# A seven-product matrix step starts two feature tiles earlier in the second layer, its right factors handed over one by one

## Chip, core and metric

The kernel runs on one core of one Trainium2 chip. The metric is device time in microseconds (us) from launch to end, and the median of several runs is compared. The engines are named as in the profile: PE is TensorE (PEld its weight loads), DVE is VectorE, ACT is ScalarE, POOL is GpSimd, and SP issues most of the loads.

## What is computed

Two layers of a backbone over 512 latent tokens and 256 context tokens, 1024 features wide; the second layer keeps the latent tokens only. Each layer has a mixer part (not touched here) and this feed-forward part, where `h` is the normed and modulated stream:

```python
D_FF = 2816
def conv_ffn(h, w_up, conv_w, w_down):
    up = h @ w_up
    a, b = up[..., :D_FF], up[..., D_FF:]
    return (jax.nn.silu(dwconv3(a, conv_w)) * b) @ w_down
```

All of it is float32, and the kernel keeps that precision: every operand of a large product is split into a high and a low part, `hi` and `lo`, and a product is three passes, hi·hi, lo·hi and hi·lo.

## The kernel before

Features lie on the partitions, tokens run along the free axis. The 2816 hidden features are 22 tiles of 128 (`f` = 0 to 21). Each tile needs its `a` rows and its `b` rows of `w_up`: two weight units of 128 x 1024 numbers, one for `a` and one for `b`.

**A plain tile.** One unit is 8 blocks of the contraction x 3 passes = 24 matmuls of 512 columns. ACT casts the unit's high part (`wh`, line 276), DVE or POOL subtracts to get the low part (`wl`, lines 286 and 288). Behind the product `a`, `gate`/`up_a` run the convolution (two DVE instructions, line 302) and the SiLU on ACT; behind `b` DVE multiplies (line 286), and `hidden` splits the result into `hi` (ACT) and `lo` (DVE).

**A quad.** Two neighbouring tiles together are a 2 x 2 block product, which `quad` (line 629) does with seven half-size products in place of eight: 7 products x 4 blocks `q` of the contraction x 3 passes = 84 matmuls of 256 columns for `a`, 84 for `b`. The left factors are sums of the weights, made by `split_quad` (line 614): four DVE additions `wr<-wr` of 128 x 512, and the high and low parts of four units (`.0` to `.2` of 1024 columns, `.3` of 512, named `s4h` and `s4l`). The right factors are made by `right_factors` (line 584) once per layer from the modulated stream: for each of the four `q`, `t13` and `t24` are sums of quarters (four DVE instructions of 256 columns), `t24` is split into `th` and `tl` (factors t2 and t4), half of `t13` into `t3`. Three factors are parts of `h2` as they are (b11, b21, b22). The last, t1, is split **in place** over the second half of `h2`'s first tile (`hhi`, `hlo`), so it must wait until no plain tile reads that half any more. `quad` uses them in the order b11, t2, t1, t3, b21, b22, t4.

Which tiles are plain is `PLAIN` (line 1856): the first layer starts quads at `f` = 4, the second at 6. The second layer's four first units (`f` = 0, 1) run as one batch in two halves while the stream is still being made; then come the plain tiles one after the other, then the quads. The down projection of a finished chunk comes one chunk later.

**What sets the order.** A scheduler (`Sched`, line 81) runs at build time. Strands of work (Python generators) yield instructions; it keeps a model of when each engine is free, and lets the strand with the lowest priority number go first among those that are ready. Each engine's order in the program is the result and is fixed on the chip. `K.when` holds a strand until its condition is true at build time. `PRF` (line 1845) is the priority of `right_factors` for each layer; splitting of weights has 2, the convolutions and multiplications 1. A low part that may go to DVE or POOL goes where the model ends it earlier.

There are 5 buffers each for `wh` and `wl` and 4 for the raw units, so a unit can be cast only when the unit five before it is done.

Of the kernel before, what the change touches and what calls it, by code (L numbers as in the profile page):

```python
# [54 lines left out]
def quads(l, f):  # L55

    return l in QUADS and f >= PLAIN[l]

# [386 lines left out]
def build(tc, a, out):  # L445
    nc = tc.nc
    es = ExitStack()
    with es:
# [9 lines left out]
        K = Sched(nc)  # L458
# [319 lines left out]
        def passes(w, h):  # L778
            return ((w[0], h[0]), (w[0], h[1]), (w[1], h[0]))
# [544 lines left out]
        def layer(l):  # L1324
# [3 lines left out]
            T = SEQ if last else TOK  # L1328
# [218 lines left out]
            quad_b, quad_t = {}, {}  # L1547
# [34 lines left out]
            H = T // 2  # L1582

            def right_factors():

                for q in range(4):
                    (hi1, lo1), (hi2, lo2) = h2[2 * q], h2[2 * q + 1]
                    yield from K.when(lambda: all((2 * q + i, g[0]) in h2.done for i in range(2) for g in halves))
                    if BACT:
                        yield from K.when(lambda: all(len(wholes.get(2 * q + i, ())) == 2 for i in range(2)))  # L1590
                        b1, b2 = wholes[2 * q][0], wholes[2 * q + 1][0]
                    else:
                        b1 = yield from S.get("b1")
                        yield from K.tt(b1[:, 0:T], hi1[:, 0:T], lo1[:, 0:T], ALU.add, ("pool",))
                        b2 = yield from S.get("b2")
                        yield from K.tt(b2[:, 0:T], hi2[:, 0:T], lo2[:, 0:T], ALU.add, ("pool",))
                    t13 = yield from S.get("t13")
                    yield from K.tt(t13[:, 0:H], b1[:, 0:H], b1[:, H:T], ALU.subtract)
                    yield from K.tt(t13[:, H:T], b1[:, H:T], b2[:, H:T], ALU.subtract)
                    S.put(b1)  # L1600
                    t24 = yield from S.get("t24")
                    yield from K.stt(t24[:, 0:H], t13[:, 0:H], -1.0, b2[:, H:T], ALU.mult, ALU.subtract)
                    yield from K.tt(t24[:, H:T], b2[:, 0:H], t24[:, 0:H], ALU.add)
                    S.put(b2)
                    th = yield from S.get("th", F32R)
                    tl = yield from S.get("tl", F32R)
                    yield from K.split(th[:, 0:T], tl[:, 0:T], t24[:, 0:T])
                    S.put(t24)
                    t3 = yield from S.get("t3", F32R)
                    yield from K.split(t3[:, 0:H], t3[:, H:T], t13[:, H:T])  # L1610
                    quad_t[q] = (t13, th, tl, t3)
                yield from K.when(lambda: state.get("plain") == l)
                for q in range(4):
                    t13, th, tl, t3 = quad_t[q]
                    (hi1, lo1), (hi2, lo2) = h2[2 * q], h2[2 * q + 1]
                    yield from K.split(hi1[:, H:T], lo1[:, H:T], t13[:, 0:H])
                    S.put(t13)
                    quad_b[q] = dict(b11=(hi1[:, 0:H], lo1[:, 0:H]), t1=(hi1[:, H:T], lo1[:, H:T]),
                                     b21=(hi2[:, 0:H], lo2[:, 0:H]), b22=(hi2[:, H:T], lo2[:, H:T]),
                                     t2=(th[:, 0:H], tl[:, 0:H]), t4=(th[:, H:T], tl[:, H:T]), t3=(t3[:, 0:H], t3[:, H:T]))  # L1620
                quad_t["free"] = [t for q in range(4) for t in quad_t[q][1:]]

            def product(bank, w, off, b, first):
                for q in range(4):
                    yield from K.when(lambda: q in quad_b)
                    yield from K.mms([(bank[:, 0:H], wp[:, off + 128 * q:off + 128 * q + 128], bp, first and q == 0 and i == 0,
                                       q == 3 and i == 2) for i, (wp, bp) in enumerate(passes(w, quad_b[q][b]))], not first)

            def quad(key, post):

                at, bk = set(), {}

                def prod(bank, w, off, b, name, first):
                    if first:
                        bk[bank] = yield from P.get(bank, 1)
                    yield from product(bk[bank], w, off, b, first)
                    at.add(name)
                K.spawn(post(bk, at), 1)
                g0 = yield from unit(key + ".0")
                yield from prod("x", g0, 0, "b11", "p1", True)  # L1640
                g1 = yield from unit(key + ".1")
                yield from prod("y", g1, 512, "t2", "p6", True)
                yield from prod("z", g1, 0, "t1", "p5", True)
                unit_done(g1)
                g2 = yield from unit(key + ".2")
                yield from prod("w", g2, 0, "t3", "p7", True)
                yield from K.when(lambda: "x read" in at)
                yield from prod("x", g0, 512, "b21", "p2", False)
                unit_done(g0)
                g3 = yield from unit(key + ".3")  # L1650
                yield from K.when(lambda: "z read" in at)
                yield from prod("z", g3, 0, "b22", "p3", False)
                S.put(*g3)
                yield from K.when(lambda: "w read" in at)
                yield from prod("w", g2, 512, "t4", "p4", False)
                unit_done(g2)
# [74 lines left out]
            if l in QUADS:  # L1731
                K.spawn(right_factors(), PRF[l])

# [108 lines left out]
STRICT = True  # L1842
PAL = 3.5
BACT = True
PRF = (1.5, 2.5)
MB0 = 3
AVALL = True
SWC = 0.09
# [4 lines left out]
EARLY = True  # L1853
RLQ = ('pool',)
ADAG = 2
PLAIN = (4, 6)
PADA = 2
ENDCTX = False
LA = 4
# [137 lines left out]
```

## Time and profile before

| | us |
|---|---|
| median of 3 runs | 1461.02 |
| lowest and highest run | 1459.94 and 1463.81 |
| the profiled execution, its own time | 1462.63 |
| its span in the profile | 1460.9 |

The span runs from the first to the last instruction in the profile; the execution's own time has 1.7 us more around it. In the timeline rows the first number is the start in us from the span's start, the second the time until the instruction has ended. Instructions of one engine overlap at their ends, so what one costs a busy engine is the distance from its start to the next one's start.

### The profile page before, as it was taken

The page shows a single profiled execution, that of the slowest core. Times are in us where ns is not written, and L with a number is a line of the kernel's source. Part 1 is how long each engine was busy: PE and PEld are TensorE (multiplying, and loading weights), DVE is VectorE, ACT ScalarE, POOL GpSimd, SP SyncE. Part 2 cuts the span into 40 slices and gives each one's busy share as a digit, 9 for nine tenths or more (in the row PEclk, how much of TensorE's full clock was granted, in tenths as well). Part 3 has the DMA queues.
Part 4 walks back from the last instruction along what each step waited for, and adds up shares of the span by engine and source line. Part 5 has one row for each costly group of instructions (what it writes and reads, how often), then busy time and mean ns, then how long its engine had stood idle before and what let it go on. Part 6 is the DMA issues. An engine that isn't in the chain of part 4 may idle for free.

```text
span 1460.9 us, 23874 instructions
## 1 busy us (share of the span) xinstructions
PE 1414.9 (97%) x9196; PEld 1265.8 (87%) x9196; DVE 1119.2 (77%) x1899; ACT 754.5 (52%) x1216; POOL 369.7 (25%) x456
## 2 busy tenths in 40 slices
PE   6999999999999999999999999998999999999997
PEld 4877888788898999999999988876789899999987
DVE  4748578767997788897777878798886767778885
ACT  5446456425543455454545444647646456656652
POOL 0231453111212122211222114476220012221130
PEclk9999999999999999999999999999999999999998
DMA  9495152224046588656886834434242267787771
GB/s 373 152 319 180 50 145 70 91 84 162 30 144 152 140 214 204 178 154 200 225 214 189 285 126 138 144 116 154 78 144 75 90 140 152 177 182 171 171 203 59
DMA packets 75538, 229.12 MB, mean 157 GB/s; under 512 B 10624, under 2 KB 12800, under 8 KB 75296
## 3 DMA queue, kind: packets, MB, share of 16 engines
q0 software_dynamic: 36256, 103.44, 29.9%
q1 hardware_dynamic: 36576, 121.67, 24.6%
q10 hardware_dynamic: 2592, 2.49, 0.5%
q8 instruction: 72, 1.18, 0.3%
q14 instruction: 42, 0.34, 0.1%
HBM read 164.64 MB, written 51.38 MB: 148 GB/s over the span
## 4 chain that ended last, share of the span: by engine, by line
PE 83%; DVE 7%; DMA 4%; issue 3%; POOL 1%; ACT 1%; SPq 0%; DVEq 0%; POOLq 0%; ACTq 0%
PE banks L234 82%; DMA adaw<-in_w_ada 2%; PE banks L247 2%; DVE mx L328 1%; DVE wl L286 1%; DMA stk<-rhi 1%; DMA x<-in_xT 0%; DVE shuf L286 0%; DMA wr<-in_w_dn 0%; DVE ropey L286 0%; POOL p L317 0%; DVE p L302 0%; POOL avr L1056 0%; DVE mlo L286 0%; DVE by L302 0%
## 5 line engine op out<-in xcount | busy, mean ns | idle before, releaser
L234 PE MATMUL banks<-hhi,wh 128*128 128x512 f32 (+2 forms) x968 | 301.3, 335 | 1.3 <-DVE oT L286 1.1
L276 ACT CAST wh<-wr 128x1024 fp32r<-128x1024 f32 x220 | 229.2, 1046 | 139.9 <-PE banks L234 85.2
L234 PE MATMUL banks<-hlo,wh 128*128 128x512 f32 (+2 forms) x968 | 298.5, 333 | 0.4 <-DVE hlo L302 0.3
L234 PE MATMUL banks<-hhi,wl 128*128 128x512 f32 (+2 forms) x968 | 297.7, 332 | 0.0
L286 DVE TENSOR_TENSOR wl<-wr,wh 128x1024 fp32r<-128x1024 f32 x189 | 230.5, 1222 | 74.2 <-ACT wh L276 61.6
L216 POOL DMA_DIRECT2D xacc<-ev x128 | 111.3, 870 | 364.0 <-ACT ev L315 359.6
L234 PEld LDWEIGHTS banks<-hhi,wh 128*128 128x128 f32 x968 | 173.1, 189 | 19.1 <-issue 3.4
L234 PEld LDWEIGHTS banks<-hlo,wh 128*128 128x128 f32 x968 | 173.2, 189 | 15.7 <-DVE hlo L302 2.6
L234 PEld LDWEIGHTS banks<-hhi,wl 128*128 128x128 f32 x968 | 173.0, 189 | 14.1 <-DVE wl L286 0.3
L234 PE MATMUL banks<-lo,wh 128*128 128x512 f32 (+1 forms) x560 | 171.0, 347 | 3.8 <-DVE lo L286 3.8
L234 PE MATMUL banks<-hi,wh 128*128 128x512 f32 (+1 forms) x560 | 171.3, 348 | 0.0
L234 PE MATMUL banks<-hi,wl 128*128 128x512 f32 (+1 forms) x560 | 170.2, 346 | 0.0
L315 ACT ACTIVATE ev<-banks,ada 128x512 f32<-128x512 f32 x192 | 111.6, 616 | 82.1 <-PE banks L234 58.8
L234 PEld LDWEIGHTS banks<-lo,wh 128*128 128x128 f32 x560 | 96.2, 190 | 18.1 <-DVE lo L286 5.1
L234 PEld LDWEIGHTS banks<-hi,wh 128*128 128x128 f32 x560 | 96.4, 189 | 13.8 <-ACT hi L276 0.2
L234 PEld LDWEIGHTS banks<-hi,wl 128*128 128x128 f32 x560 | 96.1, 189 | 14.1
L288 POOL TENSOR_TENSOR wl<-wr,wh 128x1024 fp32r<-128x1024 f32 (+1 forms) x31 | 77.4, 2504 | 117.0 <-ACT wh L276 89.6
L286 DVE TENSOR_TENSOR wr<-wr 128x512 f32<-128x512 f32 x136 | 91.1, 694 | 3.7 <-DMA wr<-in_w_up 3.0
L203 POOL DMA_DIRECT2D adaw<-in_w_adaT x56 | 34.2, 623 | 220.2 <-DVE adaw L302 158.7
L234 PE MATMUL banks<-th,wl 128*128 128x384 f32 (+1 forms) x272 | 84.4, 310 | 0.0
L234 PE MATMUL banks<-tl,wh 128*128 128x384 f32 (+1 forms) x272 | 84.4, 310 | 0.0
L234 PE MATMUL banks<-th,wh 128*128 128x384 f32 (+1 forms) x272 | 84.3, 310 | 0.0
(240 smaller groups left out, 3064.5 us busy)
## 6 DMA issues: line engine op xcount, KB each, us to landing
wr<-in_w_up SPq DMA_DIRECT2D x88, 512.0 KB, 3.8
adaw<-in_w_adaT POOLq DMA_DIRECT2D x56, 512.0 KB, 6.5
xacc<-ev POOLq DMA_DIRECT2D x64, 384.0 KB, 9.8
wr<-in_w_dn SPq DMA_DIRECT2D x44, 512.0 KB, 6.3
xacc<-ev POOLq DMA_DIRECT2D x64, 256.0 KB, 7.8
adaw<-in_w_ada SPq DMA_DIRECT2D x40, 384.0 KB, 7.6
wr<-in_w_zt SPq DMA_DIRECT2D x24, 512.0 KB, 5.0
wr<-in_w_o SPq DMA_DIRECT2D x16, 512.0 KB, 3.5
```

The source lines that it names most:

```text
L203: yield from self.op([(q, cost[q], lambda q=q: eng[q].dma_start(out, in_)) for q in queues], outs, ins)
L216: yield from self.op([("pool", 0.9, lambda: self.nc.gpsimd.dma_start(out, in_, accum_op=ALU.add))], [], [in_])
L234: self.nc.tensor.matmul(o, l, r, start=a, stop=b, skip_group_check=more)
L247: self.nc.tensor.transpose(o, i, ident)
L276: opts.append(("act", 0.19 + n / 1200, lambda: self.nc.scalar.copy(out, in_)))
L286: opts.append(("dve", 0.15 + n / 960, lambda: self.nc.vector.tensor_tensor(out, a, b, op=op)))
L288: opts.append(("pool", 0.1 + n * 2.25e-3, lambda: self.nc.gpsimd.tensor_tensor(out, a, b, op=op)))
L315: emit = dict(act=lambda: self.nc.scalar.activation(out, a, AF.Copy, scale=s), dve=lambda: self.nc.vector.tensor_scalar(out, a, s, None, o ...
L328: lambda: self.nc.vector.tensor_reduce(out, in_, axis=AX.X, op=op), [out], [in_])
```

## The change

Three edits:

- `quad_b[q]` is filled as soon as the factors of `q` are made, all but t1; t1 is added after its split in place. `product` waits for the one factor it needs, not for all.
- `PRF` of the second layer falls from 2.5 to 1, ahead of the splitting of weights.
- `PLAIN` of the second layer falls from 6 to 4: tiles 4 and 5 become the first quad, right behind plain tile 3.

```diff
                     quad_t[q] = (t13, th, tl, t3)
+                    quad_b[q] = dict(b11=(hi1[:, 0:H], lo1[:, 0:H]), b21=(hi2[:, 0:H], lo2[:, 0:H]),
+                                     b22=(hi2[:, H:T], lo2[:, H:T]), t2=(th[:, 0:H], tl[:, 0:H]),
+                                     t4=(th[:, H:T], tl[:, H:T]), t3=(t3[:, 0:H], t3[:, H:T]))
                 yield from K.when(lambda: state.get("plain") == l)
...
                     S.put(t13)
-                    quad_b[q] = dict(b11=(hi1[:, 0:H], lo1[:, 0:H]), t1=(hi1[:, H:T], lo1[:, H:T]),
-                                     b21=(hi2[:, 0:H], lo2[:, 0:H]), b22=(hi2[:, H:T], lo2[:, H:T]),
-                                     t2=(th[:, 0:H], tl[:, 0:H]), t4=(th[:, H:T], tl[:, H:T]), t3=(t3[:, 0:H], t3[:, H:T]))
+                    quad_b[q]["t1"] = (hi1[:, H:T], lo1[:, H:T])
...
-                    yield from K.when(lambda: q in quad_b)
+                    yield from K.when(lambda: b in quad_b.get(q, ()))
...
-PRF = (1.5, 2.5)
+PRF = (1.5, 1)
...
-PLAIN = (4, 6)
+PLAIN = (4, 4)
```

In the built program nothing moves in the first layer: all engines have the same instructions in the same order up to the second layer's feed-forward part, and again from its second quad on. Between them three places matter.

On VectorE, in the second layer's feed-forward part, behind the batch of tiles 0 and 1 (`fy<-banks,vec` is the convolution of an `a` tile, `fy<-banks,fy` the multiplication with a `b` tile, `wl` a low part of a weight unit, `t13`/`t24` the sums for the right factors). Before:

```order
L302 SCALAR_TENSOR_TENSOR fy_10993<-banks_77,vec_81,fy_10993 128x511 x2
L286 TENSOR_TENSOR wl_11007<-wr_10575,wh_10996 128x1024
L302 SCALAR_TENSOR_TENSOR fy_10995<-banks_77,vec_81,fy_10995 128x511 x2
L286 TENSOR_TENSOR fy_10993<-banks_77,fy_10993 128x512
L286 TENSOR_TENSOR wl_11034<-wr_10692,wh_11006 128x1024
L286 TENSOR_TENSOR lo_11040<-fy_10993,hi_11039 128x512
L286 TENSOR_TENSOR fy_10995<-banks_77,fy_10995 128x512
L286 TENSOR_TENSOR wl_11053<-wr_10728,wh_11033 128x1024
```

and with the change, from the same convolution on:

```order
L302 SCALAR_TENSOR_TENSOR fy_11012<-banks_77,vec_81,fy_11012 128x511 x2
L286 TENSOR_TENSOR tl_11011<-t24_11007,th_11010 128x512
L302 SCALAR_TENSOR_TENSOR fy_11014<-banks_77,vec_81,fy_11014 128x511 x2
L286 TENSOR_TENSOR t13_11041<-x4_9945 128x256
L286 TENSOR_TENSOR t13_11041<-x4_9945,x5_9950 128x256
L302 SCALAR_TENSOR_TENSOR t24_11051<-t13_11041,x5_9950 128x256
L286 TENSOR_TENSOR t24_11051<-x5_9950,t24_11051 128x256
L286 TENSOR_TENSOR fy_11012<-banks_77,fy_11012 128x512
L286 TENSOR_TENSOR fy_11014<-banks_77,fy_11014 128x512
L286 TENSOR_TENSOR tl_11059<-t24_11051,th_11058 128x512
L286 TENSOR_TENSOR t3_11080<-t13_11041,t3_11080 128x256
```

The three low parts that VectorE made here for the units `b` of tile 2 (`wr_10575`), `a` of tile 3 (`wr_10692`) and `b` of tile 3 (`wr_10728`) are gone from this stretch; the factor work of `q` = 1 and 2 stands in their place. Eleven rows further down, behind the factor work of `q` = 3, the third of them follows, and from there to the low halves of the factor split in place stand:

```order
L302 SCALAR_TENSOR_TENSOR fy<-banks,vec,fy 128x511 x2
L286 TENSOR_TENSOR fy<-banks,fy 128x512
L286 TENSOR_TENSOR wl<-wr,wh 128x1024
L286 TENSOR_TENSOR lo<-fy,hi 128x512
L286 TENSOR_TENSOR wl<-wr,wh 128x1024
L286 TENSOR_TENSOR wr<-wr 128x512 x4
L286 TENSOR_TENSOR wl<-wr,wh 128x1024
L302 SCALAR_TENSOR_TENSOR fy<-banks,vec,fy 128x511 x2
L286 TENSOR_TENSOR wl<-wr,wh 128x1024
L286 TENSOR_TENSOR s4l<-wr,s4h 128x512
L286 TENSOR_TENSOR wl<-wr,wh 128x1024
L286 TENSOR_TENSOR hlo<-t_10991,hhi 128x256
```

The first `wl` of these rows is the low part for `b` of tile 3 (`wr_10728`), the second unit `.0` of the first quad, `wr<-wr x4` the additions for that quad, and the next `wl`, `wl` and `s4l` its units `.1` to `.3`; the last `wl` is unit `.0` of the quad's `b` half. `hlo` is the first low half of t1. Before it stood behind the matmuls of a down projection, now it stands behind plain tile 3 with no other work of PE than the first two products of the quad between them.

On GpSimd, in the same place, between the last write of the stream and the first addition of the down projection:

```order
 L203 DMA xacc_80<-x_9964 128x256
 L203 DMA xacc_80<-x_9969 128x256
-L288 TENSOR_TENSOR wl<-wr,wh 128x1024
+L288 TENSOR_TENSOR t_11030<-t_11004,t_11030 128x256
+L288 TENSOR_TENSOR wl<-wr,wh 128x1024 x2
+L288 TENSOR_TENSOR hlo<-t_11087,hhi 128x256
 L216 DMA xacc_80<-ev 128x512 x64
```

GpSimd made one low part here (for `a` of tile 4); now it makes the low part of `t3` for `q` = 1, then the low parts for `b` of tile 2 and `a` of tile 3, then the last low half of t1.

## Rows read from the trace of the kernel before

**Rows 1.** The page: the span, busy time by engine, the chain that ended last
```profile
span 1460.9 us, 23874 instructions
PE 1414.9 (97%) x9196; PEld 1265.8 (87%) x9196; DVE 1119.2 (77%) x1899; ACT 754.5 (52%) x1216; POOL 369.7 (25%) x456
PE 83%; DVE 7%; DMA 4%; issue 3%; POOL 1%; ACT 1%; SPq 0%; DVEq 0%; POOLq 0%; ACTq 0%
```
**Rows 2.** Timeline of PE: first plain tile, first down projection, first quad, next down projection
```profile
1117.46 0.40 PE L234 MATMUL banks<-hhi,wh 128*128 128x512 f32 x1
...
1161.85 0.40 PE L234 MATMUL banks<-hi,wh 128*128 128x512 f32 x1
...
1184.11 0.28 PE L234 MATMUL banks<-hhi,wh 128*128 128x256 f32 x1
...
1187.27 0.28 PE L234 MATMUL banks<-hhi,wh 128*128 128x256 f32 x1
1187.63 0.39 PE L234 MATMUL banks<-hlo,wh 128*128 128x256 f32 x1
...
1204.21 0.40 PE L234 MATMUL banks<-hi,wh 128*128 128x512 f32 x1
```
**Rows 3.** Timeline of DVE behind the batch, and where it made right factors
```profile
1117.32 1.53 DVE L302 SCALAR_TENSOR_TENSOR fy<-banks,vec,fy 128x511 f32<-128x511 f32 x2 [5.06 <-ACT fy L266]
1118.77 1.22 DVE L286 TENSOR_TENSOR wl<-wr,wh 128x1024 fp32r<-128x1024 f32 x1
1119.90 1.53 DVE L302 SCALAR_TENSOR_TENSOR fy<-banks,vec,fy 128x511 f32<-128x511 f32 x2
...
1132.33 0.69 DVE L286 TENSOR_TENSOR tl<-t,th 128x512 fp32r<-128x512 f32 x1
1132.93 0.42 DVE L286 TENSOR_TENSOR t<-t,t 128x256 fp32r<-128x256 f32 x1
1133.26 0.42 DVE L286 TENSOR_TENSOR t<-x 128x256 f32<-128x256 f32 x1
```
**Rows 4.** Timeline of ACT in the same stretch
```profile
1116.59 0.69 ACT L266 ACTIVATE fy<-banks,vec 128x512 f32<-128x512 f32 x1 [5.92 <-PE banks L234]
1117.18 1.04 ACT L276 CAST wh<-wr 128x1024 fp32r<-128x1024 f32 x1
...
1120.22 0.63 ACT L266 ACTIVATE fy<-fy 128x512 f32<-128x512 f32 x1
...
1126.82 0.61 ACT L276 CAST th<-t 128x512 fp32r<-128x512 f32 x1
1130.10 0.40 ACT L276 CAST t<-t 128x256 fp32r<-128x256 f32 x1
```
**Rows 5.** POOL: one form (count, busy us, mean ns, idle); POOL and DVE in time
```profile
L288 POOL TENSOR_TENSOR ss<-ss,sq 128x256 f32<-128x256 f32 x4 | 2.9, 729 | 60.4 <-ACT sq L266 60.3
...
1126.01 1.53 DVE L302 SCALAR_TENSOR_TENSOR fy<-banks,vec,fy 128x511 f32<-128x511 f32 x2
1126.05 2.40 POOL L288 TENSOR_TENSOR wl<-wr,wh 128x1024 fp32r<-128x1024 f32 x1 [34.84 <-ACT wh L276]
```
**Rows 6.** Timeline of DVE and POOL where both subtract from SBUF
```profile
891.02 3.41 POOL L288 TENSOR_TENSOR wl<-wr,wh 128x1024 fp32r<-128x1024 f32 x1
892.05 2.92 DVE L286 TENSOR_TENSOR ropey<-ropey,shuf 128x512 f32<-128x512 f32 x1
...
958.57 4.95 POOL L288 TENSOR_TENSOR wl<-wr,wh 128x1024 fp32r<-128x1024 f32 x2
961.18 2.88 DVE L286 TENSOR_TENSOR shuf<-shuf,sin 128x512 f32<-128x512 f32 x1
```
**Rows 7.** Stretches by engine (us, PE, PEld, DVE, ACT, POOL busy, PEclk, DMA share, GB/s)
```profile
1085.00:1092.00 7.00, 4.58 (x45) 4.21 (x43) 6.44 (x15) 5.54 (x11) 1.84 (x4) 0.93 0.46 164
1092.00:1098.00 6.00, 6.00 (x27) 5.74 (x28) 3.88 (x8) 2.14 (x6) 0.00 (x0) 0.51 0.56 182
```
**Rows 8.** Timeline of PE: the matmul in front of that stretch, with the wait
```profile
1091.56 0.44 PE L234 MATMUL banks<-ss,mats 128*32 128x64 f32 x8 [2.42 <-DVE ss L286]
```

## The prediction

> **What bounds the kernel now.** I read the page first: TensorE is busy for 97% of the span, and the chain that ended last is TensorE for 83% [rows 1]. So time is won where TensorE has less to do, and lost where it waits. Next I read TensorE's timeline around the change. From 1117.46 to 1161.85 us it runs the second layer's eight plain units (tiles 2 to 5) without a gap: 44.39 us, 5.549 us for a unit and 0.231 us for each of its 24 matmuls. The first quad takes from 1184.11 to 1204.21, 20.10 us for 168 matmuls [rows 2]. In it one matmul starts 0.36 us behind the one in front, where 0.118 is usual (1187.27 and 1187.63): it waited 0.25 us for the low half of the factor that is split in place. Without that wait a quad takes 19.85 us. Then I read VectorE and ScalarE, which make what TensorE needs: at 1117.32 VectorE comes out of 5.06 us of idleness, and then it works closely packed [rows 3]. A small fall in its pace is hidden; a delay of several us isn't.
>
> In the first layer the change moves nothing, so handing the factors over early is worth nothing there: the places of the instructions are the same. All of it is decided between 1110 and 1165 us.
>
> **What TensorE saves.** Removed: tiles 4 and 5, four units of 5.549 us, 22.20 us. Added: one quad, 19.85 us. Gain 2.35 us. The old quad's wait of 0.25 goes too, because its in-place split is long done by then: **2.60 us**. The down projections and the other eight quads stay, and the loads on SP's queue keep their order and sizes. That sum holds if TensorE is fed as before.
>
> **What VectorE needs, and when.** The costs as distance between starts [rows 3]: a convolution 1.45 us (two instructions), a low part `wl` 1.13 (1.22 until its result is there), a 512-column instruction 0.60, a 256-column one 0.33; the four that make `t13` and `t24` take 1.46, since two wait for each other. On ScalarE a convolution's first step or a SiLU takes some 0.6, a cast 0.94, 0.61 or 0.40 by size [rows 4].
>
> The idle time up to 1117.3 now takes the factors of q = 0 and the sums of q = 1; that costs nothing. Then, in the new order: convolution (to 1118.77), `tl` (1119.37), convolution (1120.82). Meanwhile ScalarE has made the first convolution step from 1116.59, a cast, `th`, the second convolution step and the high part of t3: 1116.59 + 0.59 + 0.94 + 0.53 + 0.59 + 0.40 = 1119.6. GpSimd takes its low part (as 256 columns, 0.73 us) and right behind it the low part for `b` of tile 2 (2.40 us): 1120.4 to 1122.8 [rows 5]. TensorE needs that at 1117.46 + 5.55 + 2 x 0.23 = 1123.5, so it is in time by 0.7.
>
> **But VectorE isn't free in that time.** At 1120.8 its next instruction is a subtraction of two SBUF tensors, and GpSimd is inside one. What then happens is in the trace: at 892.05 such a VectorE instruction took 2.92 us, and one at 961.18 2.88, for 512 columns that take 0.69 [rows 6, 3]. Both times it ended 0.6 us behind GpSimd's instruction, so it had stood until that was through; and GpSimd's took 3.41 instead of 2.40 when it came second [rows 6, 5]. A convolution, which has one operand in PSUM, isn't slowed and doesn't slow GpSimd: 1.53 and 2.40 us side by side at 1126 [rows 5]. So VectorE stands from 1120.8 to 1122.8 (2.0 us), and again when GpSimd takes the low part for `a` of tile 3, which ScalarE has cast at about 1123.0: 2.4 us more. The four sums end at 1122.8 + 2.4 + 1.46 = 1126.7.
>
> The Trainium skill says in GPSIMD Engine Reference (section Specifications) that GpSimd shares its SBUF interfaces with VectorE and that VectorE instructions with two SBUF inputs contend; it doesn't say that one stands for the whole of the other. If the two only shared, each at half pace, VectorE would by my estimate lose some 1.5 us here and not 4.4, TensorE would wait 1.8 us at the split in place, and the sum would be -0.8. Rows 6 show the whole instruction waited out, and the measurement decides.
>
> From there: two multiplications (1.2), `tl` and the wait for ScalarE's cast (0.6 + 0.5), t3 (0.33), the sums of q = 3 (1.55), two `lo` (1.2), `tl` (0.6), t3 (0.33), convolution (1.53 until its end), SiLU on ScalarE with both hand-overs (0.7), multiplication (0.6), and only then the low part for `b` of tile 3 (1.22): 1126.7 + 10.4 = **1137.1**. TensorE wants it at 1117.46 + 3 x 5.549 + 0.46 = 1134.57. Before it was made ahead of all factor work. **TensorE waits 2.5 us.**
>
> VectorE goes on without a pause: `lo` 0.6, `wl` 1.13, four additions 2.4, `wl` 1.13, convolution 1.45, `wl` 1.13, `s4l` 0.6, `wl` 1.13, together 9.6 us, then the first low half of t1: 1146.6 + 0.42 = 1147.0. Without any wait TensorE would want it in the third product, at 1139.66 + 24 x 0.118 + 0.1 = 1142.6. That is 4.4 us late, of which 2.5 are waited already. The last two of the four low halves come from both engines, and one of them waits for the other's 0.73 us. So behind the third product TensorE is late by 4.4 + 0.7 = **5.1 us**. After that it isn't late again: the quad's next need of VectorE lies three products, 4 us, further on, and the down projection behind it gives VectorE slack.
>
> **Sum without the clock:** 5.1 - 2.6 = 2.5 us slower.
>
> **The clock.** After a wait of 2.42 us at 1091.56 the granted clock of the stretch 1092 to 1098 was 0.51, so 1.2 GHz where it is 2.4 otherwise [rows 8, 7]. At half pace 6 us of it lose 3. A wait of 2.5 us for `b` of tile 3 can do the same, or nothing: the bounds are 0 and 3 us. Most of it is hidden: TensorE would come to the third product at 1142.6 + 2.5 + 3 = 1148.1 and find its factors ready at 1147 to 1148.5, so it is late by 5.5 and not by 5.1 + 3. I take 0.4 us more, and keep 0 and 3.
>
> **2.5 + 0.4 = 2.9 us slower:** from the profiled execution's 1462.63 us that is 1465.5, and from the median of the runs, which is 1.6 lower, 1461.02 + 2.9 = **1463.9 us**. About 0.3%, 4.4 us, is what can be told from no change here; this is under it.
>
> **The rivals.**
>
> *The gain comes.* GpSimd and VectorE don't meet, because one of them starts a little earlier or later or because the waits are shorter than in rows 6. Then the chain on VectorE is 4.2 us earlier: the low part for `b` of tile 3 is ready at 1132.9, in time by 1.7, the first low half of t1 at 1142.9, late by 0.3. The time is 1461.0 - 2.6 + 0.3 = 1458.7 us. For it: there is 5.06 us of idleness that the factors now fill [rows 3]. Against: GpSimd's start at 1120.4 hangs on ScalarE alone, whose rows up to there are known, and VectorE's next free instruction comes 0.4 us later. Chance 0.2. Even this doesn't reach 4.4 us.
>
> *Slower for good: the clock falls behind the second wait.* The price of the clock is hidden only if it falls at the first wait. Where TensorE keeps 2.4 GHz through the first wait and then stands another 2 to 2.6 us at the third product, a fall there has no wait to hide in: 5.1 + 3 - 2.6 = 5.5 us, 1466.5 us. It decides if two waits within 13 us are followed by a granted clock near 0.5 behind the second alone. For it: 2.42 us sufficed once [rows 8, 7]. Against: the first wait is as long as the second. Chance 0.18.
>
> *Nothing comes of it* because something other than TensorE sets the end, a load or the additions of the last down projection: 1461.0. Against it stands the share of TensorE in the chain [rows 1]. Chance 0.04.
>
> **How the numbers follow.** My forecast has 0.58, and its own range is 1462.0 to 1465.2 (the clock at 0, the waits half a us shorter, or both longer by 0.8). Most of it and the first and third rival lie within 4.4 us of before: 0.56 + 0.18 + 0.04, so 0.78. Slower by more is the second rival and the end of the forecast, 0.18 + 0.02 = 0.20. Faster by more would need a gain that no term has: 0.02, taken from the first rival. The range reaches from the first rival, 1458.6, to the second, 1466.6.
>
> **What would show it.** Right: in the changed profile a wait of TensorE of 1.5 to 3 us near 1134.6, ended by `wl` of VectorE; VectorE's 256-column sums near 1120.9 and 1123.2 lasting 2 us and more, beside two instructions of GpSimd; a second wait near 1145, ended by `hlo`; a granted clock below 1 between 1137 and 1155; the first quad of the layer starting 2.5 us or more behind 1139.7. Wrong: the sums at 0.42 us each, or TensorE without a gap from 1117 to 1160; then the first rival holds. If the waits are there but the end comes earlier than 1462, something behind the first quad gave time back, and the step that says so (not late again) is wrong.

## The result, and the profile after

| | before | changed |
|---|---|---|
| median, first comparison (4 runs each) | 1460.90 us | 1469.85 us |
| ratio, first comparison | | 1.0052 [1.0037, 1.0068] |
| median, measured once more (35 and 12 runs) | 1463.08 us | 1467.87 us |
| ratio, measured once more | | 1.0034 [1.0020, 1.0048] |
| span of the profiled execution | 1460.9 us | 1468.0 us |

The changed kernel is slower, by 5 us (1461 x 0.0034) to 7.6 us (1461 x 0.0052); the medians themselves lie 4.8 and 9.0 us apart. The forecast was 2.9 us slower, 1463.9 us, and the upper end of its range 1466.6.

The page of the changed kernel: the span, the busy times, and the group of TensorE's matmuls that start a unit (busy us, mean ns | idle time before them, and what ended it):

```profile
span 1468.0 us, 24063 instructions
PE 1415.3 (96%) x9268; PEld 1270.1 (87%) x9268; DVE 1134.3 (77%) x1919; ACT 758.9 (52%) x1223; POOL 373.8 (25%) x459
...
L234 PE MATMUL banks<-hhi,wh 128*128 128x512 f32 (+2 forms) x960 | 297.0, 334 | 6.9 <-DVE fy L302 5.6
```

Against [rows 1] TensorE is busy for as long as before (1415.3 and 1414.9 us) in a span 7.1 us longer. One wait of 5.6 us stands out, and its releaser is new: `fy` of L302, a convolution. TensorE's timeline tells where. It answers to [rows 2]:

```profile
1116.91 0.40 PE L234 MATMUL banks<-hhi,wh 128*128 128x512 f32 x1
...
1127.81 0.39 PE L234 MATMUL banks<-hhi,wl 128*128 128x512 f32 x1
1133.77 0.77 PE L234 MATMUL banks<-hhi,wh 128*128 128x512 f32 x1 [5.57 <-DVE fy L302]
1134.33 0.63 PE L234 MATMUL banks<-hlo,wh 128*128 128x512 f32 x1
...
1147.11 0.28 PE L234 MATMUL banks<-hhi,wh 128*128 128x256 f32 x1
...
1166.90 0.39 PE L234 MATMUL banks<-hi,wh 128*128 128x512 f32 x1
...
1189.12 0.28 PE L234 MATMUL banks<-hhi,wh 128*128 128x256 f32 x1
...
1209.00 0.40 PE L234 MATMUL banks<-hi,wh 128*128 128x512 f32 x1
```

Two plain units run without a gap (1116.91 to 1128.2). The first matmul of the third, `a` of tile 3, then stands for 5.57 us. It reads a high part of the weights that ScalarE had made by 1122.5; what it waited for is the convolution that empties a PSUM bank (the row names its releaser; the run with another bank, below, shows that it was the bank). Behind the wait the matmuls follow each other at 0.43 us instead of 0.23. The first quad runs from 1147.11 to 1166.90, 19.79 us, without a wait.

VectorE and GpSimd in the same stretch, two timelines:

```profile
1120.28 2.33 DVE L286 TENSOR_TENSOR t<-x 128x256 f32<-128x256 f32 x1
1122.52 0.42 DVE L286 TENSOR_TENSOR t<-x,x 128x256 f32<-128x256 f32 x1
1122.86 2.63 DVE L302 SCALAR_TENSOR_TENSOR t<-t,x 128x256 f32<-128x256 f32 x1
...
1132.09 1.53 DVE L302 SCALAR_TENSOR_TENSOR fy<-banks,vec,fy 128x511 f32<-128x511 f32 x2
1134.37 0.69 DVE L286 TENSOR_TENSOR fy<-banks,fy 128x512 f32<-128x512 f32 x1 [0.76 <-ACT fy L266]
1134.98 1.22 DVE L286 TENSOR_TENSOR wl<-wr,wh 128x1024 fp32r<-128x1024 f32 x1
...
1146.80 1.09 DVE L286 TENSOR_TENSOR hlo<-t,hhi 128x256 fp32r<-128x256 f32 x3
```

```profile
1119.91 2.41 POOL L288 TENSOR_TENSOR wl<-wr,wh 128x1024 fp32r<-128x1024 f32 x1
1122.61 2.60 POOL L288 TENSOR_TENSOR wl<-wr,wh 128x1024 fp32r<-128x1024 f32 x1 [0.29 <-POOL wl L288]
```

Two sums of 256 columns take 2.33 and 2.63 us beside GpSimd's two low parts, 4.12 us more than twice 0.42. The convolution of `a` of tile 2 comes behind all that at 1132.09 and has left its bank at 1133.6; TensorE goes on at 1133.77.

Stretches of the changed kernel (us, PE, PEld, DVE, ACT, POOL busy, PEclk, DMA share, GB/s):

```profile
1128.20:1133.80 5.60, 0.04 (x1) 0.07 (x1) 5.35 (x11) 2.44 (x5) 0.00 (x0) 0.80 0.00 0
1133.80:1138.20 4.40, 4.40 (x11) 3.47 (x12) 3.83 (x5) 2.00 (x3) 0.00 (x0) 0.50 0.21 54
1138.20:1147.10 8.90, 8.90 (x39) 7.21 (x38) 8.00 (x11) 5.68 (x9) 0.00 (x0) 0.99 0.39 124
```

For 4.4 us behind the wait the granted clock is 0.50, that is 1.2 GHz; this costs 2.2 us.

**A measure for the experiments.** TensorE's instructions up to the first plain unit are the same in all kernels here, yet in their profiled executions that unit starts anywhere between 1111.7 and 1123.3 us. So the run times scatter by several us for reasons that lie ahead of the change. Within one execution I therefore also read the *stretch*: from the first matmul of the first plain unit (1117.46 before, 1116.91 after) to the first matmul of the down projection behind the quad of tiles 6 and 7 (1204.21 [rows 2] and 1209.00). It holds the same six tiles in all kernels. From there to the last block (it begins with the last quad's first matmul, at 1400.76 before) the time is 196.48 to 196.58 us in every kernel. The stretch is read from one execution of each kernel. The one kernel with two profiles has 92.09 and 91.34, so a difference of some tenths of a us between two kernels is not shown by it.

Before the stretch is 86.75 us. Without any wait the change would make it 86.75 - 2.60 = 84.15. It is 92.09: 84.15 + 5.57 (wait) + 2.2 (clock) + 0.2. The profile's 7.1 us are then 5.34 in the stretch, 2.30 in the last block (62.44 against 60.14), and 0.55 less ahead of both.

### The profile page after: what moved, and what is told of

It is laid out like the page before. It is cut to its first block, busy times and chain, and to the rows that moved or that the text cites. A ratio compares the mean times of both kernels' runs of the same rounds, so it can differ in the third digit from the quotient of the medians.

```text
span 1468.0 us, 24063 instructions
## 1 busy us (share of the span) xinstructions
PE 1415.3 (96%) x9268; PEld 1270.1 (87%) x9268; DVE 1134.3 (77%) x1919; ACT 758.9 (52%) x1223; POOL 373.8 (25%) x459
## 4 chain that ended last, share of the span: by engine, by line
PE 65%; issue 17%; DVE 7%; POOL 5%; DMA 5%; ACT 1%; SPq 0%; POOLq 0%; DVEq 0%; ACTq 0%
PE banks L234 63%; POOL xacc L216 4%; DMA adaw<-in_w_ada 2%; PE banks L247 2%; DVE mx L328 1%; DMA wr<-in_w_dn 1%; DMA xacc<-ev 1%; DMA x<-in_xT 0%; DVE shuf L286 0%; POOL p L317 0%; DMA stk<-rlo 0%; DVE p L302 0%; DVE ropey L286 0%; DVE wl L286 0%; DVE mlo L286 0%
## 5 line engine op out<-in xcount | busy, mean ns | idle before, releaser
L234 PE MATMUL banks<-hhi,wh 128*128 128x512 f32 (+2 forms) x960 | 297.0, 334 | 6.9 <-DVE fy L302 5.6
L234 PE MATMUL banks<-hlo,wh 128*128 128x512 f32 (+2 forms) x960 | 294.1, 331 | 0.3 <-DVE hlo L302 0.3
L234 PE MATMUL banks<-hhi,wl 128*128 128x512 f32 (+2 forms) x960 | 293.1, 330 | 0.0
L286 DVE TENSOR_TENSOR wr<-wr 128x512 f32<-128x512 f32 x144 | 96.3, 694 | 4.7 <-DMA wr<-in_w_up 3.9
L234 PE MATMUL banks<-th,wl 128*128 128x384 f32 (+1 forms) x288 | 89.0, 309 | 0.0
L234 PE MATMUL banks<-tl,wh 128*128 128x384 f32 (+1 forms) x288 | 88.8, 308 | 0.0
L234 PE MATMUL banks<-th,wh 128*128 128x384 f32 (+1 forms) x288 | 88.8, 308 | 0.0
```

The costliest lines, as they stand in the source:

```text
L234: self.nc.tensor.matmul(o, l, r, start=a, stop=b, skip_group_check=more)
L286: opts.append(("dve", 0.15 + n / 960, lambda: self.nc.vector.tensor_tensor(out, a, b, op=op)))
```

## The experiments

Theory A: TensorE stood for a PSUM bank, and the fall of the clock is the consequence. Theory B: the collisions of VectorE with GpSimd are the loss, whatever the bank. Theory C: the early start of the quads loses, not the order of VectorE's work. All stretches and ratios stand in one table at the end of this section. The times in the expectations start from 1461 us for the kernel before; beside these runs it had medians of 1462.0 to 1463.4 us. So I read an expected time as a distance from the kernel before, and compare it with the ratio.

**Another bank.** The planner gives a unit a bank whose pair neighbour is taken (line 406 of the changed kernel). For `a` of tile 3 that was the one that the convolution of `a` of tile 2 was to free, while three banks that had been free for over 30 us by the planner's own clock lay idle. In the kernel before, the planner had given it another bank than `a` of tile 2, one that was free in time: the new order changed the bank too. The edit prefers a bank that has long been free, for the plain units of the second layer (`l` = 1 in the code) alone. This is its main line; the others pass `soon` on:

```diff
-            c = [((b ^ 1) in self.free, t, b) for b, t in self.free.items()]
+            c = [(soon and t > self.K.T["pe"] - 8, (b ^ 1) in self.free, t, b) for b, t in self.free.items()]
```

On every engine the order of instructions stays the same; only banks differ, those of later products too.

> The changed kernel, every engine's order of instructions the same; only the third and later plain units of layer 1 take a PSUM bank that has long been free instead of the one that the convolution of a of tile 2 still reads. Theory A (the 5.57 us at 1133.77 is a wait for that bank, and the half-level clock behind it is its consequence): TensorE goes on at about 1128.2; the next thing late is the low part of b of tile 3 (1136.2 us after the change, wanted at 1134.2), a wait of about 2 us, then perhaps the low half of the in-place split (0 to 2.6 us). In all 3.5 to 6 us faster than the changed kernel: 1464 to 1466.5 us, still slower than before. Theory B (VectorE standing behind GpSimd for 4.1 us is the cause whatever the bank): the order of VectorE is the same, so the loss stays, 1468 to 1471 us.

Measured: 1465.53 us, 1.0013 [0.9998, 1.0029]. Timeline of PE, all waits of the stretch:

```profile
1137.79 0.50 PE L234 MATMUL banks<-hhi,wl 128*128 128x512 f32 x1 [2.05 <-DVE wl L286]
...
1147.89 0.39 PE L234 MATMUL banks<-hlo,wh 128*128 128x256 f32 x1 [0.18 <-DVE hlo L286]
1149.11 0.39 PE L234 MATMUL banks<-hlo,wh 128*128 128x256 f32 x1 [0.23 <-DVE hlo L286]
```

The wait for the convolution is gone, though VectorE's sums still take 2.31 and 2.62 us. So the wait was for the bank: A's mechanism is shown, and B in its strict form (no gain without a change on VectorE) falls. But the stretch falls only from 92.09 to 88.98, because the next thing is late: the low part of `b` of tile 3.

**The low parts on VectorE.** GpSimd keeps only the 0.74 us difference:

```diff
-                yield from K.tt(lo[:, 0:n], src, hi[:, 0:n], ALU.subtract, wl_engine() or ("dve", "pool"))
+                yield from K.tt(lo[:, 0:n], src, hi[:, 0:n], ALU.subtract, ("dve",) if key in ("ua1.2", "ub1.2", "ua1.3", "ub1.3") else wl_engine() or ("dve", "pool"))
```

> The changed kernel, with the low parts of the four plain units of tiles 2 and 3 all on VectorE, so that GpSimd runs only the 0.74 us difference beside the factors. Theory B (the two times that VectorE stands behind GpSimd, 1.9 and 2.2 us, are the loss): no two-operand sum of 256 columns lasts over 0.5 us, and nearly all of the loss goes, 1461 to 1463 us. Theory A (the bank): the convolution of a of tile 2 comes 4.1 us earlier less one added low part of 1.13 us, so it ends near 1130.7 instead of 1133.7; the wait of 5.57 us shrinks to 2 to 3 us and stays a wait for that convolution; 1465 to 1467.5 us.

Measured: 1463.83 us, 1.0008 [0.9993, 1.0022]. Two of the sums that collided and the convolution (DVE timeline), then all waits of the stretch (PE timeline), then the 27.6 us from the first plain unit on, in this kernel and in the one before (us, PE, PEld, DVE, ACT, POOL busy, PEclk, DMA share, GB/s):

```profile
1120.86 0.42 DVE L286 TENSOR_TENSOR t<-x 128x256 f32<-128x256 f32 x1
...
1121.53 0.42 DVE L302 SCALAR_TENSOR_TENSOR t<-t,x 128x256 f32<-128x256 f32 x1
...
1129.20 1.53 DVE L302 SCALAR_TENSOR_TENSOR fy<-banks,vec,fy 128x511 f32<-128x511 f32 x2
```

```profile
1124.79 0.50 PE L234 MATMUL banks<-hhi,wl 128*128 128x512 f32 x1 [1.12 <-DVE wl L286]
...
1130.87 0.47 PE L234 MATMUL banks<-hhi,wh 128*128 128x512 f32 x1 [0.69 <-DVE fy L302]
...
1131.91 0.51 PE L234 MATMUL banks<-hhi,wl 128*128 128x512 f32 x1 [0.34 <-DVE wl L286]
```

```profile
1117.40:1145.00 27.60, 25.45 (x119) 20.20 (x118) 27.33 (x43) 18.40 (x30) 0.73 (x1) 1.00 0.23 77
```

```profile
1117.40:1145.00 27.60, 27.60 (x122) 22.43 (x122) 24.64 (x39) 18.03 (x26) 2.40 (x1) 1.00 0.47 153
```

The same sums take 0.42 us once GpSimd is out, so the collision is shown too. The stretch is 87.10: of the 5.34 us that it had lost, 4.99 are back. That is what B had expected, nearly the whole loss gone (its 1461 to 1463 us are 0 to 2 over the kernel before, and the ratio gives 1.2). A's size was wrong: it had put the bank's wait at 2 to 3 us and the time at 4 to 6.5 over. What is left are waits of 1.12 and 0.34 us for low parts and 0.69 for the bank. So bank and collisions are links of one chain: the collisions delay VectorE, and the bank is where TensorE meets the delay. VectorE is now busy for 27.33 of 27.60 us; 2.3 us of that are the two low parts that GpSimd made in the changed kernel.

**Both.** The free bank and the low parts on VectorE.

> The free bank and the low parts on VectorE together. Theory A plus B as two parts of one chain (collisions make VectorE late, the bank and the low part are where TensorE meets it): the bank wait of 0.69 us that was left goes too, but the low parts of b of tile 2 and of a of tile 3 are still wanted before VectorE has them, 1 to 3 us of waits for low parts in all, the first quad 2.5 to 4 us behind the ideal 22.2 us after the first plain unit; time within 1.5 us of the kernel with the low parts on VectorE alone (1463.8). If the two losses were independent, the gains would add up to 4.4 + 6.1 us and the kernel would come 1.5 to 3 us under the kernel before.

Measured: 1464.91 us, 1.0008 [0.9996, 1.0021], stretch 87.10 again. The bank's wait is gone; in its place TensorE waits 1.12 and 1.28 us for low parts. The gains don't add up, as the expectation had it.

**One edit at a time.** First, the changed kernel with the old priority:

```diff
-PRF = (1.5, 1)
+PRF = (1.5, 2.5)
```

> Early hand-over and four plain tiles, but the factors keep their old low priority 2.5. Theory A says that the factors' work ahead of the convolutions made the loss, so with the old priority the plain tiles run without the bank wait (none over 1 us between 1117 and 1139), but the factors come late: the first quad then stands behind them, several us at its second or third product. 1464 to 1474 us; the sign against the changed kernel is what the run tells. A theory C (it is the early start of the quads alone that loses, not the order of the factors) would have the same loss as the changed kernel, 1468 to 1471.

Measured: 1473.61 us, 1.0078 [1.0057, 1.0100]. Timeline of PE, the waits of the stretch:

```profile
1144.26 0.58 PE L234 MATMUL banks<-th,wh 128*128 128x256 f32 x1 [4.11 <-ACT th L276]
...
1147.44 0.58 PE L234 MATMUL banks<-th,wh 128*128 128x256 f32 x1 [1.65 <-ACT th L276]
...
1150.67 0.58 PE L234 MATMUL banks<-th,wh 128*128 128x256 f32 x1 [1.71 <-ACT th L276]
```

The plain units run without a wait (first quad 22.22 us behind the first plain unit), then the quad waits 7.5 us for factors; with a granted clock of 0.53 from 1145 to 1158 the stretch is 97.69. So the early start of the quads does lose by itself where the factors keep their old place, and more than the changed kernel (C had expected the same loss), but by another wait. C for the changed kernel is tested by the run with six plain tiles, the next but one. Then the early hand-over alone:

```diff
-PRF = (1.5, 1)
+PRF = (1.5, 2.5)
...
-PLAIN = (4, 4)
+PLAIN = (4, 6)
```

> The early hand-over alone: six plain tiles, priority 2.5, that is the kernel before but for each product's wait. Theories A, B and C: the factors are all made before the first quad begins, so only the last in-place splits can be waited for less; within 0.5 us of the kernel before, 1460 to 1461.5 us, the old wait of 0.25 us at the first quad gone.

Measured: 1462.27 us, 0.9996 [0.9981, 1.0010], the stretch 86.99, as expected but for one thing: the old small wait isn't gone, it is 0.34 us, now for a low half from GpSimd. Then priority 1 with six plain tiles:

```diff
-PLAIN = (4, 4)
+PLAIN = (4, 6)
```

> The priority 1 of the factors and the early hand-over with six plain tiles as before, so no quad is gained and none starts earlier. Theory A with VectorE's queue as the root (factor work put ahead of what the next plain units need): TensorE waits 3 to 6 us in the plain stretch between 1123 and 1135, here for the low part of a of tile 3, which the new order has behind all factors on VectorE; 3 to 6 us slower than before. Theory C (the early start of the quads is what loses): no loss, within 1 us of the kernel before.

Measured: 1466.70 us, 1.0027 [1.0013, 1.0041]. Timeline of PE:

```profile
1131.91 0.50 PE L234 MATMUL banks<-hhi,wl 128*128 128x512 f32 x1 [3.52 <-DVE wl L286]
```

and of DVE, the first of four sums, and the low part behind the factor work:

```profile
1121.73 0.41 DVE L286 TENSOR_TENSOR t<-x 128x256 f32<-128x256 f32 x1
...
1130.64 4.62 DVE L286 TENSOR_TENSOR wl<-wr,wh 128x1024 fp32r<-128x1024 f32 x4
```

As A expected: the priority alone loses 5.05 us of the stretch, with no quad in it that starts earlier, so C falls. There is no collision in this kernel either (the sums take 0.41 us, and GpSimd makes no low part there), and `a` of tile 3 has another bank than `a` of tile 2. The order of VectorE's work is enough for a loss; the collisions and the bank are what it meets in the changed kernel. And last the changed kernel without the hand-over: `quad_b[q]` is filled as before.

> The changed kernel without its first edit: the factors are handed over all together after the split in place, as before; priority 1 and four plain tiles stay. Theory A (the loss is made on VectorE ahead of the third plain unit, long before any product): TensorE's order is the same, the wait of 5 to 6 us at the third plain unit stays, the stretch from the first plain unit to the end of the second quad is 91 to 94 us, 1.003 to 1.006 of the kernel before. Theory G (the early hand-over moves the loss): the wait is under 3 us or the stretch under 90 us.

Measured: 1467.93 us, 1.0047 [1.0029, 1.0065], the wait 5.56 us, the stretch 91.42. Handing over early does nothing that shows in either kernel.

**The changed kernel once more.**

> The changed kernel itself once more, beside the others on one chip: theories A and B alike 1.004 to 1.007 of the kernel before (1466 to 1472 us by the base of this chip), with the wait of 5 to 6 us at the third plain unit, ended by the convolution. What it tells apart is the end stage: if the wait of 0.56 us for a high half there and the second half-level piece of the clock come back, they belong to the kernel; if not, to the run.

Measured: 1.0034 [1.0020, 1.0048], a little under the range. The wait at the third plain unit is there to the hundredth:

```profile
1131.30 0.77 PE L234 MATMUL banks<-hhi,wh 128*128 128x512 f32 x1 [5.57 <-DVE fy L302]
```

The last block takes 60.85 us, 62.44 in the first profile and 60.14 before. The wait of 0.56 us for a high half isn't back here, but it is in the kernel without the hand-over (0.82). The low clock behind the waits there is back for half as long: 0.59 from 1428 to 1432, where the first profile has 0.56 and 0.58 over 1428 to 1436. The kernel before has 0.70 from 1424 to 1428.

**Is VectorE's queue too long, or only in the wrong order?** Theory D: its length is what TensorE waits for now. E: the rest is TensorE's own. F: only the order (and the collisions) are wrong. One kernel takes work away; it leaves out VectorE's subtractions for the low halves of t2 and t4, writes a copy in their place on ScalarE, and so doesn't compute the same (the lines stand in `right_factors`, which begins at line 1584 of the kernel before, not 584; `quad` begins at 1629):

```diff
-                    yield from K.split(th[:, 0:T], tl[:, 0:T], t24[:, 0:T])
+                    yield from K.copy(th[:, 0:T], t24[:, 0:T], ("act",))
+                    yield from K.copy(tl[:, 0:T], t24[:, 0:T], ("act",))
```

> Changes part of the computation: the low halves of the eight t2 and t4 factors of layer 1 are written by ScalarE as plain copies, in place of VectorE's four subtractions of 128x512 (0.61 us each on its queue); else the free bank and the low parts on VectorE. Theory D (with the bank and the collisions out of the way VectorE's own queue is what TensorE waits for in this stretch): 2.4 us less on VectorE; the stretch from the first plain unit to the end of the second quad falls from 87.1 us to 84.5 to 86 us (84.15 is the time without any wait), 1 to 2.5 us under the kernel before. Theory E (the rest of the loss is TensorE's own, say the start of a quad or its clock): the stretch stays at 86.8 to 87.3 us and the time within 1 us of the kernel before.

Measured: 1462.78 us, 0.9998 [0.9983, 1.0013], stretch 86.32. Of the 2.95 us that were missing at 87.10 (against 84.15) the 2.4 us of VectorE gave back 0.8. No wait is left in the plain units, but two come up in the first quad:

```profile
1142.71 0.38 PE L234 MATMUL banks<-hlo,wh 128*128 128x256 f32 x1 [0.65 <-DVE hlo L286]
...
1154.09 0.39 PE L234 MATMUL banks<-t,wl 128*128 128x256 f32 x1 [0.75 <-DVE wl L286]
```

That is less than D expected and more than E allows. It is one profile, and ScalarE has four copies more, so it doesn't say how much of the 2.95 us is VectorE's length. A second kernel, with the free bank too, only reorders: the low parts of `b` of tile 2 and of tile 3 run at priority 0.95, ahead of all else (a generator of its own for these three keys, with the same subtraction on VectorE).

> The free bank, and the low parts of b of tile 2 and of tile 3 go to VectorE ahead of the factors and the convolutions. Theory D: the plain units wait for nothing (first quad 22.2 to 22.6 us after the first plain unit), but VectorE's queue is as long as before, so 2 to 3 us of waits come back inside the first quad or behind it, and the stretch ends at 86.3 to 87.5 us, the time within 1.5 us of the kernel before. Theory F (only the order of VectorE's queue is wrong, not its length): the stretch ends at 84.2 to 85 us, 2 to 3 us under the kernel before.

Measured: 1464.69 us, 1.0008 [0.9993, 1.0023]. The plain units wait for nothing (first quad at 22.23 us), and the waits come back in the first quad, now for the low parts of the quad's own units:

```profile
1144.46 0.38 PE L234 MATMUL banks<-th,wl 128*128 128x256 f32 x1 [0.98 <-DVE wl L286]
...
1159.60 0.38 PE L234 MATMUL banks<-t,wl 128*128 128x256 f32 x1 [1.50 <-DVE wl L286]
```

The stretch is 87.87, above D's range as well as F's. In this kernel GpSimd took a quad's low part, and VectorE stood 2.2 us behind it, so one more kernel keeps GpSimd out of the stretch:

> The kernel with the low parts first, and GpSimd out of the stretch altogether: the low half of t3, the low part of the first quad's unit and the low half of the in-place split, which GpSimd still made there, go to VectorE too. In the kernel with the low parts first VectorE stood 2.2 us and 0.4 us behind GpSimd; the three instructions add 1.8 us to VectorE. Theory D (the length of VectorE's queue decides): the stretch from the first plain unit to the end of the second quad is 86.8 to 87.5 us, about what the kernels without a collision have (87.10), no wait in the plain units, 1 to 3 us of waits inside or between the quads; time within 1.5 us of the kernel before. Theory F (order and collisions decide, not length): 84.2 to 86 us, 1 to 2.5 us under the kernel before.

Measured: 1463.88 us, 1.0016 [1.0001, 1.0031], stretch 88.70, with waits of 0.54, 0.40, 0.82 and 1.49 us in the first quad. F falls: neither the low parts first nor the absence of collisions brings the stretch below 87.10. It is above D's range too, so the length of VectorE's queue doesn't settle it alone; what the order adds here, and what the 1.8 us that VectorE took over, wasn't taken apart.

**An attempt to beat both.** Free bank, the factors' low halves on VectorE, one low part of the plain units left on GpSimd (the planner put two other subtractions there, of 1.30 and 1.58 us).

> The free bank, the factors' low halves of layer 1 all on VectorE, the low part of b of tile 2 alone on GpSimd and those of tile 3 on VectorE: an attempt to beat both kernels. Theory A: one collision of at most 2 us is left beside the transfer to GpSimd; VectorE has the low part of a of tile 3 about 2 us late; first quad 2 to 4 us behind the ideal; between 1.5 us under and 1.5 us over the kernel before. Theory B (collisions alone set the time): with one of two collisions left, 1.5 to 2.5 us over the kernel before.

Measured: 1465.64 us, 1.0020 [1.0004, 1.0035], stretch 87.19, one wait of 2.77 us for a low part. By the medians it is 2.6 us over before, just above B's range and outside A's; by the stretch 0.44 us over. Part of the difference is the last block, 61.29 us against 60.14. The same holds elsewhere: stretch and last block together give 6.4 us for the kernel without the hand-over (ratio 6.9) and 12.1 for the one with the old priority (11.4). No kernel of this study that computes the same beats the one before by more than can be measured.

| kernel | stretch, us | first quad behind the first plain unit, us | ratio to before |
|---|---|---|---|
| before / hand-over alone | 86.75 / 86.99 | six plain tiles | 1 / 0.9996 |
| priority 1, six plain tiles | 91.80 | six plain tiles | 1.0027 |
| changed, two profiles | 92.09, 91.34 | 30.20, 29.45 | 1.0052, 1.0034 |
| changed without the hand-over | 91.42 | 29.53 | 1.0047 |
| changed with the old priority | 97.69 | 22.22 | 1.0078 |
| other bank | 88.98 | 26.09 | 1.0013 |
| low parts on VectorE / with other bank | 87.10 / 87.10 | 25.21 / 25.21 | 1.0008 / 1.0008 |
| attempt | 87.19 | 25.30 | 1.0020 |
| low parts first / without GpSimd | 87.87 / 88.70 | 22.23 / 22.22 | 1.0008 / 1.0016 |
| VectorE relieved of four subtractions | 86.32 | 22.22 | 0.9998 |

## Why the prediction was wrong, by its own steps

- **TensorE saves 2.60 us.** Right as far as the profile can tell: two quads of the changed kernel take 19.79 and 19.88 us, and from the stretch to the last block the time is that of before (196.56 and 196.55 us).
- **VectorE isn't free in that time.** Right. The sums stand behind GpSimd at 1120.28 and 1122.86 (said: 1120.9 and 1123.2), and lose 1.91 and 2.21 us, 4.12 in all (said: 2.0 and 2.4). They end 0.28 us behind GpSimd's instruction; in [rows 6] it is 0.54, where the prediction has 0.6. The Trainium skill says in Trainium Architecture — The Big Picture (section What this means for kernel authors) that VectorE and GpSimd hold their shared ports by an exclusive lock, "not a bandwidth split". The trace agrees: 2.33 and 2.63 us beside GpSimd's 2.41 and 2.60, and 0.42 without it.
- **TensorE waits 2.5 us** for the low part of `b` of tile 3. **This step failed.** The low part came at 1136.2 (said: 1137.1), but TensorE never stood for it. I had listed what TensorE needs as weight parts and factors, and left out where it writes. The third plain unit had the bank that the convolution of `a` of tile 2 still had to empty, and that convolution stood in the same delayed queue, ahead of the low part. So TensorE stopped at the unit's first matmul, 5.57 us, and not 2.5 us one unit later. Before, the convolutions ran ahead of the factors ([rows 5]: the one of `a` of tile 2 at 1126.01), and the third unit had another bank. The Trainium skill has a rule that points there, in Perfetto Trace Analysis (section Matmuls): independent matmul groups should rotate through different PSUM banks, so that one is emptied while the next group runs. In the changed kernel the plain units did rotate, but between two banks, and emptying one took longer than the unit between: `a` of tile 2 ended near 1122.5 and its convolution at 1133.6, while the unit between ended at 1128.2. The run with another bank agrees: 92.09 falls to 88.98.
- **5.1 us late in all.** Wrong in the changed kernel, where TensorE is 8.0 us late at the first quad, and the split in place is hidden behind that. With another bank the step comes near: waits of 2.05, 0.18 and 0.23 us and 1.3 us for the clock (0.56 over 3 us), the stretch 88.98 - 84.15 = 4.8 us over what it could be. With the gain of 2.60 that is 2.2 us slower, where I had 2.9. The sum was that of a kernel with a free bank.
- **The clock, 0 to 3 us, mostly hidden.** The size is right (2.2 us, 1.5 in the second profile). That it is hidden is wrong in the changed kernel, because no second wait came to hide it. With another bank it fits: behind the 1.3 us of low clock the split in place was waited for 0.41 us, and not 2.6.
- **Not late again.** Not borne out: this is a second step that failed, by some 1 us. The last block takes 60.27 to 62.44 us in the kernels with four plain tiles and 59.90 to 60.42 in those with six. In the changed kernel TensorE waits there 0.56, 2.02 and 0.73 us instead of 1.71 and 1.12, and ScalarE waits 3.56, 1.25 and 0.17 us for weight loads shortly ahead of that, where it was 2.68 and 0.33. Why these loads land later, and why it differs so much between runs, stays open; no run was made on it.
- **The rivals.** That the gain comes was said to need that GpSimd and VectorE don't meet. They can be kept apart, and then the gain still doesn't come: 87.10 against 86.75. What I had not seen is how little room VectorE has: in the two plain tiles that the change removes it made part of the factors and of the next weights. In the 27.6 us from 1117.4 it is busy for 24.64 us before and 27.33 in the kernel without collisions. That this is why the gain doesn't come is not fully shown, since 2.4 us less for VectorE gave back only 0.8. The second rival's time, 1466.5, lies close to what was measured (5 to 7.6 us over before, it had 5.5). That is luck: it needed two waits and a fall of the clock behind the second, and there was one wait.

## What to carry to other kernels

When a change delays an engine, list for the engine that waits on it not only what it reads but also where it writes: a buffer handed out by a rule that takes no account of how late its reader may be turns a hidden delay into a stop. And before shortening the bound engine's work, add up what the next engine makes under its cover: here TensorE's 2.6 us didn't come even without collisions and with a free bank, and every order of VectorE's work that was tried only moved the wait.

## What was not expected of the hardware

The same wait isn't followed by the same clock. Behind 5.57 us of waiting the granted clock was 0.50 over the next 4.4 us in one profile, and 0.65 in another of the same kernel; behind 2.05 us (other bank) 0.56 over 3 us; behind 2.77 us (the attempt) it stayed at 1.00. Stretches of the second profile of the changed kernel, of the kernel with another bank and of the attempt, each from the end of the wait; the last one is the kernel with the old priority, over two of its three waits:

```profile
1131.30:1135.70 4.40, 4.40 (x13) 3.55 (x14) 3.79 (x5) 2.03 (x3) 0.00 (x0) 0.65 0.20 40
```

```profile
1138.00:1141.00 3.00, 3.00 (x9) 2.36 (x9) 2.96 (x5) 0.17 (x1) 0.00 (x0) 0.56 0.56 176
```

```profile
1126.30:1130.00 3.70, 3.70 (x16) 3.05 (x17) 3.70 (x6) 0.67 (x2) 0.00 (x0) 1.00 0.05 12
```

```profile
1145.00:1158.00 13.00, 9.33 (x38) 7.86 (x39) 8.66 (x21) 4.91 (x11) 0.73 (x1) 0.53 0.05 20
```

So what the clock adds to a wait is a range and not a number: here 0 to 2.2 us behind a single wait, and by my estimate some 4.4 us in the last row (9.33 us of work at 0.53), around waits that follow each other closely.
